# Gate and MLP modulation: from accumulated rows closed by TensorE to dot products closed on GpSimd

## The chip, the cores and the metric

The kernel runs on one NeuronCore of a Trainium2 chip. The metric is the device time of one execution in microseconds; the time before is the median of three runs. A profile holds one execution, taken by the hardware profiler; its rows name the engines PE (TensorE), PEld (TensorE's weight loads), DVE (VectorE), ACT (ScalarE), POOL (GpSimd) and SP (the queue that issues the DMAs).

## The reference, cut to what matters

One decoder block on 1024 tokens of width 1024, all in float32. A conditioning vector `c` modulates both sub-layers:

```python
cond = jax.nn.silu(c)
mod = cond @ w_ada + b_ada                     # 6 x 1024 values
sh_a, sc_a, gt_a, sh_m, sc_m, gt_m = split(mod, 6)
h = rms_norm(x, g_attn_pre) * (1 + sc_a) + sh_a
...                                            # projections, rotary, attention A and B, mixing
x = x + gt_a * rms_norm(mixed @ w_out, g_attn_post)
h = rms_norm(x, g_mlp_pre) * (1 + sc_m) + sh_m
y = square(relu(h @ w_up)) @ w_down
x = x + gt_m * rms_norm(y, g_mlp_post)
```

Attention A has 8 query heads on 2 key heads with a window of 128 and a sink; attention B has 8 heads that mix three dilated windows. Rotary turns the first 16 of each head's 64 columns. The change concerns the last four parts of `mod`: `gt_a` (needed when the attention's output is gated), `sh_m` and `sc_m` (needed before the MLP) and `gt_m` (needed at the very end), and the tables for the rotary turn.

## The kernel before, in words

TensorE's float32 products are made of three products of rounded high and low parts: every projection, output and MLP step is three 128x512 matmuls (L910, L911 and L913; L1818 to L1820; L2308 to L2310).

The work goes through these stages. At the start the first two parts of `mod` are computed and `x` is normed and transposed. Then come six units of projections, `pj`, two for attention A (`u` = 0 and 1) and four for B (`u` = 2 to 5). While the projections of one unit run, the attention of the units before runs in between: scores (`s_ps`), softmax with the largest value found on VectorE, the exponential on ScalarE (`p_sb`), the division mostly on GpSimd, transposes on TensorE (`pt_ps`), their split into high and low part on ScalarE and VectorE (`ph`), and the outputs (`o_ps`). In B units the third item of each head looks far back (`far`): it needs a regrouped copy of the queries (`q_far`, on ScalarE or GpSimd) and a chain of small VectorE operations (`st_far`, `a_far`, `d_far`, `z_far`). Then follow the output projection with gate and norm, and the MLP as seven products of a fast matrix scheme for each of eight halves.

The order of every engine's instructions is fixed when the program is written out. A planner (`Sched`) holds queues of steps with estimated durations, dependencies, and counted resources (`Res`) for buffers; it repeatedly hands out the step that can start first, ties by `prio`. Steps with two engines to choose from go where they end earlier. TensorE has named streams (`dense`, `s`, `t`, `pv`, `fin`, ...), and `dense` fills in where no attention step is ready. Each engine then executes its list strictly in order, so a step that waits holds up all behind it. The count `st.d` is the number of projection units done.

The modulation (`ada_piece`, L1035). The weights of the four parts form 8 halves of 512 columns. Each partition holds eight of the 1024 rows, and a piece takes two of these eight, so a half is 4 pieces. A piece is a load of 512 KB into a staging buffer (`stage`, 5 buffers, shared with the projections' `hl` tiles) and four GpSimd operations: each of the two rows times its value of `cond` (L1058, L1062), added to an accumulator `ada_acc` (L1063). After the fourth piece TensorE sums over the 128 partitions by a matmul with ones (stream `fin`): for the gates one 128x512 matmul (L1076), whose result VectorE adds to `b_ada` and multiplies by the gain, both loaded as 128 equal rows, and which goes to DRAM as 128 rows (`gate_d`); for `sh_m` and `sc_m` four matmuls with one column (L1079), closed by VectorE into `s_m` and `g_m`. A bank of PSUM is taken from `px` for it. The first 24 pieces (six halves) are let go one by one by `feed_ada` from `st.d` of 1.0 to 4.93; the last 8 pieces run on VectorE (L1060) during the MLP, let go by `feed_ada2`.

The rotary tables (`tables`, L735): GpSimd copies sines and cosines into a tile `rows` by small copies of 8 columns per token block (L748; 10 for each of the two tiles of the first call, 8 for each of the second), TensorE transposes them (`ptab`, L754), ScalarE scales them into `tabs`. The first call serves units 0 and 1; the second, let go when the projections of unit 2 begin, serves the B units.

Of the kernel before, what the change touches and what calls it, by code (L numbers as in the profile page):

```python
# [10 lines left out]
F32 = mybir.dt.float32  # L11
# [8 lines left out]
P = 128  # L20
# [28 lines left out]
_INS = ["x", "positions", "w_mod", "w_ada", "b_ada", "g_attn_post", "w_in", "w_out", "g_mlp_post", "w_up", "w_down"]  # L49
# [14 lines left out]
CW = CW_PK + 8  # L64
# [35 lines left out]
def _host(inputs):  # L100

    h = {n: np.ascontiguousarray(inputs[n]) for n in _INS if n != "w_mod"}
# [14 lines left out]
    h["w_mod"] = np.ascontiguousarray(w.transpose(3, 2, 4, 1, 0)).reshape(KC, 2, P, D)  # L117
    h["positions"] = np.ascontiguousarray(inputs["positions"][0].reshape(TB, P).T)
# [255 lines left out]
def hybrid_block(ctx: ExitStack, tc: tile.TileContext, x, positions, w_mod, w_ada, b_ada, g_attn_post, w_in, w_out,  # L374
                 g_mlp_post, w_up, w_down, consts, out):
# [4 lines left out]
    w_ada, w_out, w_up, w_down = w_ada[0], w_out[0], w_up[0], w_down[0]  # L380
# [57 lines left out]
    gate_d = [dram.tile([P, D], F32, name=f"gate_d{i}") for i in range(2)]  # L438
    ada_view = w_ada.rearrange("(p j) n -> p j n", j=KC)
# [40 lines left out]
    def rsqrt_mean(dst, src, deps, dur):  # L480
        box, n = [], dst.shape[-1]

        def first():
            box.append(small.tile([P, 8], F32, name="rs_t", tag="rs_t"))
# [111 lines left out]
    e_sin = op("ACT", 1.5, lambda: A.activation(small.tile([P, 8], F32, name="rs_t", tag="rs_t")[:, 0:1], ones[:, 0:1],  # L596
# [9 lines left out]
    condb, bc = p0.tile([P, D], F32, name="condb"), {}  # L606
# [128 lines left out]
    def tables(groups, place, r_place, r_bank, bank, deps):  # L735

        for i in range(2):
            b = {}

            def f_rows(i=i, b=b):  # L740
                t = b["t"] = place()[:].rearrange("p (b r) -> p b r", b=TB)
                G.memset(t, 0.0 if i else 1.0)
                for o, step, h in groups:
                    for x in range(2):
                        src = sinw[:, :, 1 - x] if i else cosw[:]
                        o_ = o + 64 * x
                        for j in range(h):
                            G.tensor_copy(t[:, :, o_ + j * step:o_ + j * step + (8 * h - h) * step + 1:h * step], src)  # L748
            e = op("POOL", 8.0 if r_place is r_wa else 4.4, f_rows, [e_rope], takes=[(r_place, 1)], prio=0)
            for x in range(2):  # L750
                def f_t(x=x, b=b):
                    b[x] = bank()
                    for j in range(4):
                        T.transpose(b[x][:, j], b["t"][:, 4 * x + j], ident)  # L754
                d = pe_op("tab", 0.43, f_t, [e], takes=[(r_bank, 1)], gives=[(r_place, 1)] if x else [])
                e_tab[x].append(op("ACT", t_ps(512) + AP_COST, lambda i=i, x=x, b=b: A.mul(
                    tabs[i][:, 512 * x:512 * x + 512], b[x][:].rearrange("p b t -> p (b t)"), scl[0]), [d] + deps[x],
                                   gives=[(r_bank, 1)], prio=2))
# [231 lines left out]
    def feed_proj():  # L990
        if len(sc.pe.get("dense", [])) <= 4 and todo_dense:
# [3 lines left out]
            if (u, x, c) == (2, 0, 0):  # L995
                for e_ in e_tab:
                    e_.clear()
# [6 lines left out]
    def open_attention():  # L1004
        if any(x.t is None for x in e_tab[0] + e_tab[1] + list(e_hl.values())):
            return False
        nonlocal kring, qring, vfring, pprob, pth, opool, adp, mask_a, mask_b, mask_n, mask_f, swap, pick, e_mask
# [9 lines left out]
        adp = pool("adp", 1, **kw)  # L1017
# [4 lines left out]
        e_mask = load(lambda: nc.sync.dma_start(masks[:], consts[:, CW_MB:CW]), 724992, prio=-20)  # L1022
        swap = [masks[:, 1152 + P * w:1152 + P * w + P] for w in range(2)]
        pick = [masks[:, 1408 + 4 * w:1412 + 4 * w] for w in range(2)]
        mask_b, mask_n = masks[:, 0:512], masks[:, 512:768]
        mask_f, mask_a = masks[:, 768:896], masks[:, 896:1152]
# [4 lines left out]
    kring = qring = vfring = pprob = pth = opool = adp = mask_a = mask_b = mask_n = mask_f = swap = pick = e_mask = None  # L1031
# [3 lines left out]
    NADA = 24  # L1035
    ada = Tok()
    ada.i, ada.acc, ada.e, ada.raw, ada.gate = 0, None, Ev(0.0), {}, {}
    e_mod = {}
    r_adacc = Res(1)

    def ada_piece(i, eng, accp, psum, r_ps, r_acc=None):
        g, jp = divmod(i, 4)
        col = 2 * D + g * 512

        def f_load():
            ada.raw[i] = stage("wa_st")
            nc.sync.dma_start(ada.raw[i][:].rearrange("p (j n) -> p j n", j=2),
                              ada_view[:, 2 * jp:2 * jp + 2, col:col + 512])
        el = load(f_load, 524288, takes=[(r_stg, 1)], prio=20)

        def f_acc():
            wa = ada.raw.pop(i)[:].rearrange("p (j n) -> p j n", j=2)
            if jp == 0:
                ada.acc = accp()
            for j in range(2):
                cj = cond[:, 2 * jp + j:2 * jp + j + 1]
                if jp == 0 and j == 0:
                    eng.tensor_scalar(ada.acc[:, :512], wa[:, 0], cj, 1.0, ALU.mult, ALU.mult)  # L1058
                elif eng is V:
                    V.scalar_tensor_tensor(ada.acc[:, :512], wa[:, j], cj, ada.acc[:, :512], ALU.mult, ALU.add)  # L1060
                else:
                    G.tensor_scalar(wa[:, j], wa[:, j], cj, 1.0, ALU.mult, ALU.mult)  # L1062
                    G.tensor_tensor(ada.acc[:, :512], ada.acc[:, :512], wa[:, j], ALU.add)  # L1063
# [3 lines left out]
        if jp < 3:  # L1067
            return
# [1423 lines left out]
```

## Time and profile before

| | |
|---|---|
| runs, us | 1094.43, 1095.38, 1095.84 (median 1095.38) |
| profiled execution, us | 1095.04 |
| its span, us | 1093.3 |
| granted TensorE clock, mean | 0.997 |
| DMA, bytes moved | 197.95 MB |

The span runs from the first to the last instruction that the profiler saw; 1.7 us of the execution lie around it. How to read the rows: a group has line, engine, operation, output and input, count, then busy time and mean ns, then the idle time before the group's instructions and what ended it. A wait row names who waited, for whom, us in total, times and longest. A timeline row has start, length, and in brackets the idle time before it. In the chain of work that ended last each step gets only the time that it adds to the chain.

### The profile page before, as it was taken

How to read it: one execution, taken by the hardware profiler on the slowest of the kernel's cores; microseconds unless marked ns; L12 is line 12 of the kernel's file. 1: busy time of each engine (PE TensorE's matmuls, PEld its weight loads, DVE VectorE, ACT ScalarE, POOL GpSimd, SP SyncE). 2: the span in 40 equal slices, each digit the busy share in tenths (PEclk: the TensorE clock that was granted, in tenths of full speed). 3: DMA queues.
4: the chain of work that ended last, by engine and by line, in shares of the span. 5: the costliest groups of instructions: out<-in, count | busy, mean ns of one | idle time of the engine just before them, and what ended most of it. 6: DMA issues, size and time to landing. Idle time of an engine off the chain costs nothing.

```text
span 1093.3 us, 15289 instructions
## 1 busy us (share of the span) xinstructions
PE 1077.9 (99%) x5254; PEld 898.1 (82%) x5254; DVE 815.7 (75%) x1430; ACT 621.8 (57%) x1155; POOL 284.3 (26%) x378
## 2 busy tenths in 40 slices
PE   8999999999999999999999999999999999999997
PEld 6888888888888888888888888888888888888885
DVE  7978776667768688699796655898746995537978
ACT  6868876455656867686755234733245632347532
POOL 3649778496846631100000000000000000000002
PEclk9999999999999999999999999999999999999999
DMA  8565656354625447368721579234687043594014
GB/s 341 212 228 154 190 170 210 138 183 141 206 102 173 142 149 267 116 231 313 278 82 39 178 254 356 89 99 145 246 302 295 1 135 119 192 330 177 29 47 185
DMA packets 90559, 197.95 MB, mean 181 GB/s; under 512 B 8560, under 2 KB 25072, under 8 KB 90480
## 3 DMA queue, kind: packets, MB, share of 16 engines
q1 hardware_dynamic: 90480, 196.95, 52.2%
q8 instruction: 42, 0.69, 0.3%
q14 instruction: 37, 0.30, 0.1%
HBM read 145.54 MB, written 32.51 MB: 163 GB/s over the span
## 4 chain that ended last, share of the span: by engine, by line
PE 94%; DVE 2%; POOL 2%; issue 1%; ACT 1%; DMA 1%; SPq 0%; POOLq 0%; DVEq 0%
PE mlp_ps L2308 19%; PE mlp_ps L2310 18%; PE mlp_ps L2309 18%; PE pj L910 5%; PE pj L913 5%; PE pj L911 5%; PE y_ps L1818 3%; PE y_ps L1819 3%; PE y_ps L1820 3%; PE o_ps L1517 2%; PE s_ps L1324 1%; PE s_ps L1229 1%; PE o_ps L1417 1%; PE pt_ps L1381 1%; PE pt_ps L1481 1%; PE acc L910 1%
## 5 line engine op out<-in xcount | busy, mean ns | idle before, releaser
L2308 PE MATMUL mlp_ps<-hw 128*128 128x512 f32 x896 | 349.6, 390 | 0.0
L2310 PE MATMUL mlp_ps<-hw 128*128 128x512 f32 x896 | 348.6, 389 | 0.0
L2309 PE MATMUL mlp_ps<-hw 128*128 128x512 f32 x896 | 348.6, 389 | 0.0
L2309 PEld LDWEIGHTS mlp_ps<-hw 128*128 128x128 f32 x896 | 168.2, 188 | 35.2 <-issue 0.5
L2308 PEld LDWEIGHTS mlp_ps<-hw 128*128 128x128 f32 x896 | 168.2, 188 | 35.2 <-issue 0.5
L2310 PEld LDWEIGHTS mlp_ps<-hw 128*128 128x128 f32 x896 | 168.2, 188 | 35.0
L2020 DVE TENSOR_TENSOR hw<-w,hw 128x1024 fp32r<-128x1024 f32 x92 | 109.9, 1221 | 83.2 <-ACT hw L2013 82.7
L2408 POOL TENSOR_TENSOR st<-st,nhalf 128x1 f32<-128x1 f32 x8 | 7.6, 956 | 611.0 <-DVE st L2405 611.0
L2013 ACT CAST hw<-w 128x1024 fp32r<-128x1024 f32 x92 | 93.6, 1049 | 122.6 <-PE mlp_ps L2310 90.3
L910 PE MATMUL pj<-hw,w_hl 128*128 128x512 f32 x240 | 102.4, 427 | 0.0
L913 PE MATMUL pj<-hw,w_hl 128*128 128x512 f32 x240 | 95.0, 396 | 0.0
L911 PE MATMUL pj<-hw,w_hl 128*128 128x512 f32 x240 | 94.7, 394 | 0.0
L2013 ACT CAST hw<-u 128x1024 fp32r<-128x1024 f32 x48 | 48.8, 1052 | 64.0 <-PE mlp_ps L2310 64.0
L2020 DVE TENSOR_TENSOR hw<-u,hw 128x1024 fp32r<-128x1024 f32 x48 | 57.1, 1220 | 17.2 <-ACT hw L2013 17.2
L2366 DVE TENSOR_TENSOR yacc<-yacc,mlp_ps 128x512 f32<-128x512 f32 x96 | 62.4, 684 | 4.5 <-PE mlp_ps L2310 4.3
L1063 POOL TENSOR_TENSOR ada_acc<-ada_acc,wa_st 128x512 f32<-128x512 f32 x42 | 55.2, 1314 | 3.5
L913 PEld LDWEIGHTS pj<-hw,w_hl 128*128 128x128 f32 x240 | 45.3, 189 | 10.3
L1818 PE MATMUL y_ps<-hw,oh 128*128 128x512 f32 x128 | 51.6, 403 | 0.0
L1819 PE MATMUL y_ps<-hw,oh 128*128 128x512 f32 x128 | 50.0, 391 | 0.0
L911 PEld LDWEIGHTS pj<-hw,w_hl 128*128 128x128 f32 x240 | 45.8, 191 | 4.4
L910 PEld LDWEIGHTS pj<-hw,w_hl 128*128 128x128 f32 x240 | 45.5, 190 | 4.5
L2347 ACT ACTIVATE u<-u 128x512 f32<-128x512 f32 x48 | 28.9, 625 | 30.9 <-DVE u L2345 30.2
(261 smaller groups left out, 1995.0 us busy)
## 6 DMA issues: line engine op xcount, KB each, us to landing
hw<-s_dram SPq DMA_DIRECT2D x84, 512.0 KB, 4.4
wa_st<-in_w_ada SPq DMA_DIRECT2D x32, 512.0 KB, 4.7
w<-in_w_up SPq DMA_DIRECT2D x32, 512.0 KB, 4.7
w<-in_w_down SPq DMA_DIRECT2D x32, 512.0 KB, 7.3
s_dram<-hw SPq DMA_DIRECT2D x28, 512.0 KB, 3.2
qt<-hl SPq DMA_DIRECT2D x40, 256.0 KB, 2.5
w_st<-in_w_in SPq DMA_DIRECT2D x36, 256.0 KB, 3.0
x_sb<-in_x SPq DMA_DIRECT2D x16, 512.0 KB, 6.0
```

The lines of the kernel that those rows point to most:

```text
L910: T.matmul(ps, w[:, 0, n], h[0], start=(k == 0), stop=False)
L911: T.matmul(ps, w[:, 1, n], h[0], start=False, stop=False)
L913: T.matmul(ps, w[:, 0, n], h[1], start=False, stop=(k == KC - 1))
L1063: G.tensor_tensor(ada.acc[:, :512], ada.acc[:, :512], wa[:, j], ALU.add)
L1818: T.matmul(ps[:], oh, wh[:, c0:c0 + 512], start=(k == 4 * m), stop=False)
L1819: T.matmul(ps[:], oh, wl[:, c0:c0 + 512], start=False, stop=False)
L2013: A.copy(out[j][0], flat(src[j]))
L2020: V.tensor_tensor(out[j][1], flat(src[j]), out[j][0].bitcast(F32), ALU.subtract)
L2308: T.matmul(ps[m][:], sh, mh, start=starts and k == 0, stop=False, **kw)
L2309: T.matmul(ps[m][:], sh, ml_, start=False, stop=False, **kw)
L2310: T.matmul(ps[m][:], sl, mh, start=False, stop=k == 3, **kw)
L2366: e = op("DVE", t_dv(512), lambda: V.tensor_tensor(y(), y(), ps[m][:], ALU.add), [e, ml.e_y[tb, n]], gives=gives, prio=-1 if (h, p) == ml. ...
```

## The change

The weights of the four parts are laid out by the host as 32 pieces of 128 partitions by 1024: a piece holds, for 128 of a part's 1024 outputs, one output per partition and its whole row of 1024 weights. The row form of `cond`, `condb`, which the start builds anyway, is kept in a pool that lives longer. A piece is now one load of 512 KB, two GpSimd products with `condb` of 512 columns each (L1052), and one ScalarE pass that copies in place and sums each row into a column of `dots` (L1057). After the eight pieces of a part, GpSimd closes it with operations on 128x8 (L1065 to L1074): adds the bias, multiplies by the gain (both now columns of the constants tile). The gates go to DRAM as one row of 1024 and are read back with every partition getting the same row. TensorE and VectorE have no part in it any more. All 32 pieces are let go between `st.d` of 2.0 and 5.29; the pieces in the MLP and the loads of biases and gains are gone.

In `tables` the copies that differ only by their place in a group become one copy with a broadcast; each copy is a step of its own, the transposes of the second call wait for the tables' last reader, and that call is let go two projections earlier, at the second projection of unit 1's second half. Several small tiles get fewer buffers (`rs_t` 3, `z_far` 1, `y_far` 1, `d_far` 2, `mn4` and `den4` 4, `rab` 2, `st2` 3, `st_l` 1).

```diff
-    NADA = 24
+    NADA = 4 * KC
...
-    def ada_piece(i, eng, accp, psum, r_ps, r_acc=None):
-        g, jp = divmod(i, 4)
-        col = 2 * D + g * 512
+    def ada_piece(i):
+        c, k = divmod(i, KC)
         def f_load():
             ada.raw[i] = stage("wa_st")
-            nc.sync.dma_start(ada.raw[i][:].rearrange("p (j n) -> p j n", j=2),
-                              ada_view[:, 2 * jp:2 * jp + 2, col:col + 512])
-        el = load(f_load, 524288, takes=[(r_stg, 1)], prio=20)
-        def f_acc():
...
-                    G.tensor_scalar(wa[:, j], wa[:, j], cj, 1.0, ALU.mult, ALU.mult)
-                    G.tensor_tensor(ada.acc[:, :512], ada.acc[:, :512], wa[:, j], ALU.add)
...
-                T.matmul(b[0][:, :512], ones[:], ada.acc[:, :512], start=True, stop=True)
-            else:
-                for k in range(4):
-                    T.matmul(b[0][:, k:k + 1], ada.acc[:, k * P:(k + 1) * P], ones[:, 0:1], start=True, stop=True)
...
+            nc.sync.dma_start(ada.raw[i][:], w_ada[c, k])
+        e = load(f_load, 524288, takes=[(r_stg, 1)], prio=20)
+        e = op("POOL", 2 * t_ptt(512), lambda: [G.tensor_tensor(ada.raw[i][:, cs], ada.raw[i][:, cs], condb[:, cs], ALU.mult)
+                                                for cs in (slice(0, 512), slice(512, D))], [e], prio=9)
+
+        def f_sum():
+            w = ada.raw.pop(i)[:]
+            A.activation(w, w, AF.Identity, accum_out=dots[:, c, k:k + 1])
+        ada.e.append(op("ACT", t_as(D) + 0.19, f_sum, [e], gives=[(r_stg, 1)], prio=9))
+        if k < KC - 1:
             return
...
+        def f_c():
+            d = dots[:, c]
+            if c == 1:
+                G.tensor_tensor(s_m[:], d, cols[:, 40:48], ALU.add)
+            elif c == 2:
+                G.tensor_tensor(g_m[:], d, b1m[:], ALU.add)
+                G.tensor_tensor(g_m[:], g_m[:], cols[:, 16:24], ALU.mult)
             else:
...
+                at = 16 if c else 0
+                G.tensor_tensor(d, d, gates[:, at:at + 8], ALU.add)
+                G.tensor_tensor(d, d, gates[:, at + 8:at + 16], ALU.mult)
+                if c:
+                    G.tensor_scalar(d, d, D ** 0.5, 1.0, ALU.mult, ALU.mult)
+        e = op("POOL", 0.3, f_c, ada.e + [e_mask], prio=4)
...
     def feed_ada():
-        if st.d > 1.0 + ada.i * 4.1 / NADA and ada.i < NADA:
+        if st.d > 2.0 + ada.i * 3.4 / NADA and ada.i < NADA:
...
     def tables(groups, place, r_place, r_bank, bank, deps):
...
-                        for j in range(h):
-                            G.tensor_copy(t[:, :, o_ + j * step:o_ + j * step + (8 * h - h) * step + 1:h * step], src)
-            e = op("POOL", 8.0 if r_place is r_wa else 4.4, f_rows, [e_rope], takes=[(r_place, 1)], prio=0)
+                    def f_rows(o=o + 64 * x, step=step, h=h, x=x, i=i, b=b):
+                        to = b["t"][:, :, o:o + (8 * h - 1) * step + 1:step].rearrange("p b (f j) -> p b f j", j=h)
+                        G.tensor_copy(to, (sinw[:, :, 1 - x] if i else cosw[:]).unsqueeze(3).to_broadcast([P, TB, 8, h]))
+                    e.append(op("POOL", 0.4 + 0.4 * h, f_rows, [es, e_rope], prio=0))
...
-            if (u, x, c) == (2, 0, 0):
+            if (u, x, c) == (1, 1, 1):
...
     def feed_ada2():
-        if ada.i < 32:
-            if ada.i >= NADA and ml.begun > 8 + 2 * (ada.i - NADA):
-                ada_piece(ada.i, V, lambda: stage("ada_acc"),
-                          lambda: px.tile([P, 512], F32, name="ada_ps", tag="x"), r_x, r_stg)
-                ada.i += 1
+        if ml.begun <= 24:
             return False
```

Where each engine's instructions stand before and after is shown with the prediction's steps.

More of the change, by code (lines that the diff above doesn't have):

```diff
@@ L100, in _host @@
 def _host(inputs):
-    h = {n: np.ascontiguousarray(inputs[n]) for n in _INS if n != "w_mod"}
+    h = {n: np.ascontiguousarray(inputs[n]) for n in _INS if n not in ("w_mod", "w_ada")}
     c = np.zeros((P, CW), np.float32)
@@ L594, in hybrid_block @@
     e = op("ACT", 0.1, lambda: A.activation(cond[:], c_raw, AF.Exp, scale=-1.0), [e_c], prio=0)
-    e_sin = op("ACT", 1.5, lambda: A.activation(small.tile([P, 8], F32, name="rs_t", tag="rs_t")[:, 0:1], ones[:, 0:1],
+    e_sin = op("ACT", 1.5, lambda: A.activation(small.tile([P, 8], F32, name="rs_t", tag="rs_t", bufs=3)[:, 0:1], ones[:, 0:1],
                                                 AF.Sin), [e, e_init], prio=0)
@@ L738, in tables, with f_set @@
             b = {}
[L740 to L746, printed above, removed]
-                        for j in range(h):
-                            G.tensor_copy(t[:, :, o_ + j * step:o_ + j * step + (8 * h - h) * step + 1:h * step], src)
-            e = op("POOL", 8.0 if r_place is r_wa else 4.4, f_rows, [e_rope], takes=[(r_place, 1)], prio=0)
+            def f_set(i=i, b=b):
+                b["t"] = place()[:].rearrange("p (b r) -> p b r", b=TB)
+                G.memset(b["t"], 0.0 if i else 1.0)
+            es = op("POOL", 1.0, f_set, [e_rope], takes=[(r_place, 1)], prio=3)
+            e = []
+            for o, step, h in groups:
+                for x in range(2):
+                    def f_rows(o=o + 64 * x, step=step, h=h, x=x, i=i, b=b):
+                        to = b["t"][:, :, o:o + (8 * h - 1) * step + 1:step].rearrange("p b (f j) -> p b f j", j=h)
+                        G.tensor_copy(to, (sinw[:, :, 1 - x] if i else cosw[:]).unsqueeze(3).to_broadcast([P, TB, 8, h]))
+                    e.append(op("POOL", 0.4 + 0.4 * h, f_rows, [es, e_rope], prio=0))
             for x in range(2):
@@ L1723, in f_set @@
             def f_set():
-                A.activation(small.tile([P, 8], F32, name="rs_t", tag="rs_t")[:, 0:1], ones[:, 0:1], AF.Sqrt)
+                A.activation(small.tile([P, 8], F32, name="rs_t", tag="rs_t", bufs=3)[:, 0:1], ones[:, 0:1], AF.Sqrt)
             op("ACT", 1.5, f_set, [e_x2[1]], prio=3)
@@ L1855, in f1 @@
             def f1():
-                t = small.tile([P, 8], F32, name="rs_t", tag="rs_t")
+                t = small.tile([P, 8], F32, name="rs_t", tag="rs_t", bufs=3)
                 bx.append(t)
@@ L1909, in f_ev @@
                 return f
[L1910 removed]
+            e = op(("DVE", "ACT"), (1.3, 1.45), (f_ev(V), f_ev(A)), [et[kg]] + [e_mod[g] for g in (1, 2)] +
                    (e_h2[q][-1:] if tq else []) + ([e_far] if tb == 0 else []),
```

127 lines of the change are left out of this document (42 added, 85 removed).

## The prediction, made before the changed kernel ran

> **What bounds the kernel now.** I read the page first (busy shares and the chain of work that ended last), then the waits of TensorE, then busy time by stretches. The page:
>
> ```profile
> span 1093.3 us, 15289 instructions
> PE 1077.9 (99%) x5254; PEld 898.1 (82%) x5254; DVE 815.7 (75%) x1430; ACT 621.8 (57%) x1155; POOL 284.3 (26%) x378
> PE 94%; DVE 2%; POOL 2%; issue 1%; ACT 1%; DMA 1%; SPq 0%; POOLq 0%; DVEq 0%
> ```
>
> TensorE is busy in 1077.9 of 1093.3 us and holds 94% of the chain. Whatever leaves its queue shortens the run, unless a wait takes its place. The waits of TensorE after the start are these (line waited at, releaser, us in total, times, longest):
>
> ```profile
> PE o_ps L1517 <- DVE ph L1497: 1.3, 1, 1.3
> PE pm_o L1776 <- DVE ph L1497: 1.0, 1, 1.0
> PE s_ps L1229 <- POOL q_far L1205: 0.8, 1, 0.8
> PE ada_ps L1079 <- POOL p_sb L1299: 0.2, 1, 0.2
> ```
>
> Only the last two fall where the change works. Busy time by stretches (length; PE, PEld, DVE, ACT, POOL; granted clock; DMA share; GB/s):
>
> ```profile
> 80.00:140.00 60.00, 60.00 (x349) 51.00 (x348) 46.78 (x139) 50.73 (x145) 49.92 (x88) 1.00 0.58 168
> 138.00:326.00 188.00, 187.03 (x1068) 159.90 (x1067) 130.98 (x390) 110.79 (x300) 134.93 (x162) 0.99 0.52 163
> 190.00:200.00 10.00, 9.40 (x52) 8.17 (x53) 4.98 (x17) 3.71 (x13) 8.37 (x9) 0.83 0.19 59
> 420.00:1080.00 660.00, 660.00 (x2941) 546.49 (x2940) 491.75 (x564) 337.61 (x477) 13.78 (x17) 1.00 0.50 179
> ```
>
> From 80 to 140 us ScalarE is 85% busy (50.73 of 60) and TensorE never waits; in the MLP (420 to 1080) it never waits either. At 190 us the 0.80 us wait is followed by a granted clock of 0.83 over 10 us, 1.7 us lost.
>
> **What the change takes off TensorE.** Each of the eight modulation halves ends in matmuls against ones. The instructions that write ada_ps, their count, minimum, median and maximum ns:
>
> ```profile
> L1079 PE MATMUL ada_ps<-ones,ada_acc x32: 164/250/250, 191.6 to 306.8; 128*128 128x1 f32 x32
> L1076 PE MATMUL ada_ps<-ada_acc,ones x8: 590/592/627, 106.8 to 781.1; 128*128 128x512 f32 x8
> ```
>
> Durations overlap in the pipeline, so I price them by the chain of waits, which gives each step only the time that it adds (start, us, what):
>
> ```profile
> 106.92 0.86 PE ada_ps L1076 x2
> 148.19 0.86 PE ada_ps L1076 x2
> 191.79 0.79 PE ada_ps L1079 x8
> 306.25 0.79 PE ada_ps L1079 x8
> 631.02 0.89 PE ada_ps L1076 x2
> 631.91 0.23 PE mlp_ps L2308
> 780.87 0.86 PE ada_ps L1076 x2
> ```
>
> The MLP matmul behind one takes its usual 0.23 us, so nothing is given back. Four row closings at 0.86, 0.86, 0.89 and 0.86 are 3.47 us; four column closings at the 0.79 of their first and last are 3.16. Together 6.63 us leave a queue that is never empty. In the program, TensorE in the fourth B unit, where s_ps are scores, o_ps outputs and pj a projection, before:
>
> ```order
> L1408 MATMUL o_ps<-ph,v_hl 128x128
> L1229 MATMUL s_ps<-kt,qt 128x256 x4
> L1079 MATMUL ada_ps<-ones,ada_acc 128x1 x4
> L910 MATMUL pj<-hw,w_hl 128x512
> L911 MATMUL pj<-hw,w_hl 128x512
> ```
>
> The same place after the change, with shifted lines; its first five rows are
>
> ```order
> L1374 MATMUL o_ps<-ph,v_hl 128x128
> L1195 MATMUL s_ps<-kt,qt 128x256 x4
> L916 MATMUL pj<-hw,w_hl 128x512
> L917 MATMUL pj<-hw,w_hl 128x512
> L919 MATMUL pj<-hw,w_hl 128x512
> ```
>
> The closing is gone and the projection follows the scores. The counts of scores, transposes and outputs behind the last projection are the same in both programs (32, 44, 60), so the attention's end has the same work to hide.
>
> **What it adds in the B units.** The 24 GpSimd pieces of before run from 82 to 304 us (L1063); their loads are let go from 1.0 to 1.0 + 23 x 4.1/24 = 4.93 units, so a unit lasts about 57 us, and the new gate (2.0 to 5.29) puts 32 pieces into about 138 to 326 us. GpSimd's additions with their first and last start, its groups (busy, mean ns, idle before), and the modulation's part between 138 and 326 us, that is of L1058, L1062 and L1063 in this order:
>
> ```profile
> L1063 POOL TENSOR_TENSOR ada_acc<-ada_acc,wa_st x42: 1278/1294/1817, 82.1 to 304.3; 128x512 f32<-128x512 f32 x42
> L1063 POOL TENSOR_TENSOR ada_acc<-ada_acc,wa_st 128x512 f32<-128x512 f32 x42 | 55.2, 1314 | 3.5
> L1062 POOL TENSOR_SCALAR wa_st<-wa_st,cond 128x512 f32<-128x512 f32 x42 | 31.4, 747 | 20.7 <-DMA wa_st<-in_w_ada 20.7
> L1315 POOL COPY p_sb<-nsink 128x4 f32<-128x4 f32 x16 | 2.9, 192 | 1.8 <-PE pt_ps L1381 1.8
> 138.00:326.00 188.00, 0.00 (x0) 3.34 (x4) 0.99 0.52 163
> 138.00:326.00 188.00, 23.26 (x31) 0.99 0.52 163
> 138.00:326.00 188.00, 41.63 (x32) 0.99 0.52 163
> ```
>
> There the modulation takes 68.2 us now (3.34 + 23.26 + 41.63). It will take 64 x 1.314 = 84.1, and eight closing operations of 128x8, put at the 0.19 us of the 128x4 copy (1.5 us; at the 1.31 of a product, 10.5). GpSimd goes from 134.9 to 134.9 - 68.2 + 85.6 = 152.3 of 188 us, 81%. ScalarE gets 32 sums; an ACTIVATE of 1024 columns with a sum beside it, and the read of the sum:
>
> ```profile
> L1849 ACT ACTIVATE junk<-y_sb 128x1024 bf16<-128x1024 f32 x14 | 14.8, 1059 | 8.0 <-DVE y_sb L1842 3.7 <-DVE y_sb L1868 2.9 <-DVE rs_t L1786 1.3
> L1849 ACT ACTIVATION_READ_ACCUMULATOR junk<-y_sb 128x1 f32 x14 | 2.7, 193 | 0.0
> ```
>
> 1.059 + 0.193 = 1.25 us, 40 us in all: ScalarE goes from 110.8 to 150.8 of 188 us, 80%, under the 85% that it bore from 80 to 140 us without a wait of TensorE. Both fit; what counts is order. ScalarE in the first B unit, where ph are the probabilities that TensorE waits for, p_sb the softmax, w_hl the next weights, before:
>
> ```order
> L1388 CAST ph<-pt_ps 128x512 [waits PE_49,Activation_49]
> L561 CAST w_hl<-w_st 128x512 [waits DMAHW5_49]
> L1187 ACTIVATE p_sb,den<-p_sb,mn 128x384 [waits DVE_49,Pool_49]
> L561 CAST w_hl<-w_st 128x512 [waits DMAHW4_49,PE_49]
> L1452 COPY otmp<-o_ps 64x512 [waits PE_49,Activation_49]
> ```
>
> and after, where L1057 is the sum:
>
> ```order
> L1354 CAST ph<-pt_ps 128x512 [waits PE_49,Activation_49]
> L1057 ACTIVATE wa_st,dots<-wa_st 128x1024 [waits DMAHW6_49,DMAHW3_49,Pool_49]
> L566 CAST w_hl<-w_st 128x512 [waits DMAHW3_49,PE_49]
> L1153 ACTIVATE p_sb,den<-p_sb,mn 128x384 [waits DVE_49]
> L1418 COPY otmp<-o_ps 64x512 [waits PE_49,Activation_49]
> ```
>
> So ScalarE now waits for a GpSimd product, which waits for a load, with softmax, ph and otmp queued behind, and TensorE waits for those. How late a product can be is bounded by what GpSimd and ScalarE waited for before:
>
> ```profile
> POOL ada_acc L1058 <- DMA wa_st<-in_w_ada: 10.1, 3, 5.6
> POOL wa_st L1062 <- DMA wa_st<-in_w_ada: 20.7, 7, 9.8
> ACT hl L798 <- POOL ada_acc L1063: 2.4, 1, 2.4
> ```
>
> GpSimd stood 30.8 us before loads, ScalarE 2.4 us behind a modulation block, and TensorE is charged with one 0.80 us wait for it. New waits of TensorE thus lie between -2.7 us (0.80, 0.17 and the clock's 1.7 vanish) and the rivals' 7.8 and 13.1. I take +1.0, near the 0.80 that is charged now: each block gets shorter (2.6 us for a product against 4.1 for a piece of two multiplications and two additions), but the pieces are more and ScalarE is tied to them.
>
> **A rule against the change.** Products with two tensor inputs can hold up VectorE. The row where a 128x16 operation takes 2.19 us while GpSimd works on a 2.39 us product, and what TensorE then waits:
>
> ```profile
> 330.33 2.39 POOL L1591 TENSOR_TENSOR hw<-wo_st,hw 128x1024 fp32r<-128x1024 f32 x1
> 330.57 2.19 DVE L1289 TENSOR_TENSOR st_far<-st_far,d_far 128x16 f32<-128x16 f32 x1
> 333.92 0.56 PE L1517 MATMUL o_ps<-ph,v_hl 128*128 128x256 f32 x3 [1.30 <-DVE ph L1497]
> ```
>
> The Trainium skill, page "SBUF — State Buffer", section "SBUF: two separate sides", says why: a VectorE operation with two SBUF inputs and a GpSimd operation exclude each other for a whole instruction. By that rule the trace agrees: both rows end within 0.05 us. The change doubles such holds in the B units, 41.6 to 84.1 us, in pieces of 1.31. Yet between 80 and 320 us no wait of TensorE is put down to VectorE with the 41.6, so it is inside my +1.0; at full price it is rival (b), 1096.2.
>
> **Edits put at nothing.** The wider rotary copies: GpSimd's first 20 copies last 6.66 + 8.06 us, and TensorE's wait before the transposes is 0.35, not put down to them:
>
> ```profile
> 28.28 6.66 POOL L748 COPY rows<-cosw 128x64 f32<-128x64 f32 x10
> 38.25 8.06 POOL L748 COPY rows<-sinw 128x64 f32<-128x64 f32 x10
> 54.63 0.63 PE L754 MATMUL ptab<-head,rows 128*128 128x128 f32 x4 [0.35 <-issue]
> ```
>
> so at most 0.35 us comes of it; if a wide copy were no faster than four narrow ones, the projections still cover it. The eight VectorE pieces leave the MLP, where VectorE is not waited for. The gate rows become a load from one row; used far later. Fewer buffers for small tiles: their next writer stands several items behind; cover gone, one reuse would cost about the 0.8 of a late operand.
>
> **The sum.** 1095.04 for the profiled execution (span 1093.3), less 6.63, plus 1.0: 1089.4 us. The median of the runs is 1095.38, 0.34 above this execution; I leave that out.
>
> **The rivals.** (a) The present waits go too: 1095.04 - 6.63 - 2.7 = 1085.7. For it: the wait at 190 us came from GpSimd running two blocks before q_far. Against: pieces stand before q_far still. (b) The holds: if each of the six far items in the stretch costs TensorE the 1.30 us seen once, 7.8 us: 1096.2. (c) The freed time in the attention turns into waits for the softmax chain, and only the two MLP closings count, 0.89 + 0.86: 1093.3. Against: projections fill TensorE there, 187.03 of 188 us. (d) The slower one: ScalarE, in order behind late products. If ten of 32 (as ten times GpSimd waited for a load) cost TensorE 0.80 us each, and three of these the clock's 1.7, it is 8.0 + 5.1 = 13.1: 1101.5. It decides from 6.63 + 2.2 = 8.8 us of new waits, 0.28 per piece. For it: the new order; against: 30.8 us of waiting cost TensorE 0.97 before.
>
> **How the numbers follow.** Chances: forecast 0.59, (a) 0.13, (b) 0.10, (c) 0.06, (d) 0.12. A measurement can tell 0.2%, 2.2 us: faster is below 1093.2 (forecast and a, 0.72), same up to 1097.6 (b and c, 0.16), slower above (d, 0.12). The range goes from 1085.0, under (a), to 1096.2, (b); it leaves out (d). The forecast's own range is 1087 to 1092.
>
> **What would show it.** Right: no ada_ps rows, TensorE's busy time down by about 6.6 us, waits of TensorE between 130 and 330 us of 1 to 4 us, the MLP without waits. Wrong: waits of ph, p_sb or otmp on ScalarE for wa_st that TensorE shows again, granted clock under 0.97 in several stretches of 10 us, or VectorE's far operations at 1 us and more with TensorE behind them.

## The result, and the profile after

The changed kernel takes 1088.98 us (median of 6 runs, 1088.14 to 1093.14) beside 1095.61 us of the kernel before (median of 6). The ratio is 0.995, with a 95% interval from 0.9939 to 0.9961: 4.3 to 6.7 us. The profiled execution took 1089.32 us, 5.72 less than the one of before.

The page of the changed kernel:

```profile
span 1087.5 us, 15255 instructions
PE 1071.9 (99%) x5214; PEld 893.5 (82%) x5214; DVE 802.7 (74%) x1397; ACT 649.8 (60%) x1208; POOL 275.0 (25%) x349
PE 95%; DVE 2%; POOL 1%; ACT 1%; issue 1%; POOLq 0%; DVEq 0%; ACTq 0%
```

TensorE has 40 matmuls fewer (5214 against 5254) and is busy 6.0 us less. Its idle time is span less busy: 15.4 us before, 15.6 after. So in this pair of profiles the whole gain stands in the busy row, and the idle time is the same in sum. A second profile of the changed kernel, `after_again` below, has 17.6 us of idle time, so differences of 2 us in it are not told apart. Its waits after the first 70 us (line waited at, releaser, us in total, times, longest):

```profile
PE pm_o L1742 <- DVE ph L1463: 1.0, 1, 1.0
PE x_far L1231 <- DVE ph L1463: 0.8, 1, 0.8
PE o_ps L1483 <- DVE ph L1463: 0.8, 1, 0.8
PE x_far L1231 <- DVE z_far L1224: 0.8, 1, 0.8
```

They add up to 3.4 us, as the four of before did to 3.3, but only the one at pm_o is the same. The waits at q_far and ada_ps are gone, and so is the hold that the prediction shows, 1.30 us at 333.92 us; in their place stand two at x_far (198.80 and 266.94 us) and one at o_ps (219.73), each 0.8 us. So the B units lost and the stretch behind them won: by stretches TensorE's idle time goes from 0.97 to 2.31 us between 138 and 326 us, and from 2.51 to 1.19 us between 326 and 420. Busy time by stretches (length; PE, PEld, DVE, ACT, POOL; granted clock; DMA share; GB/s), the last two rows being two short stretches:

```profile
80.00:140.00 60.00, 60.00 (x356) 51.57 (x355) 45.70 (x136) 49.79 (x136) 33.41 (x64) 1.00 0.36 109
138.00:326.00 188.00, 185.69 (x1055) 158.24 (x1054) 135.33 (x392) 143.38 (x363) 151.35 (x170) 1.00 0.61 203
420.00:1080.00 660.00, 659.41 (x2939) 546.36 (x2937) 482.56 (x553) 334.86 (x475) 15.64 (x19) 1.00 0.47 169
190.00:200.00 10.00, 9.23 (x56) 7.92 (x55) 8.60 (x26) 7.79 (x24) 8.69 (x7) 1.00 0.24 74
380.00:390.00 10.00, 10.00 (x54) 8.48 (x54) 7.63 (x12) 5.67 (x9) 4.49 (x8) 0.86 0.35 115
```

GpSimd is busy 151.35 of the 188 us of the B units and ScalarE 143.38, and TensorE still works 185.69 of them. The clock's dip stands at 380 us instead of 190 us, at about the same price: 1.4 us for 1.7. In after_again no stretch of 10 us between 70 and 430 us has one, so it comes and goes between executions of one kernel. The groups of the modulation (busy us, mean ns of one, idle before it):

```profile
L1052 POOL TENSOR_TENSOR wa_st<-wa_st,condb 128x512 f32<-128x512 f32 x64 | 82.2, 1307 | 24.8 <-DMA wa_st<-in_w_ada 21.4 <-issue 3.4
L1057 ACT ACTIVATE wa_st<-wa_st 128x1024 f32<-128x1024 f32 x32 | 33.9, 1059 | 17.5 <-POOL wa_st L1052 17.5
```

The durations are those that the rows of before gave, and ScalarE does stand behind products, 17.5 us in all. The three waits of the B units show what that and the holds of VectorE do here. Two are holds (start, us, what, in brackets the idle time before it):

```profile
194.92 2.54 POOL L1052 TENSOR_TENSOR wa_st<-wa_st,condb 128x512 f32<-128x512 f32 x2
196.29 2.45 DVE L1224 TENSOR_TENSOR z_far<-st_far,masks 128x32 f32<-128x32 f32 x2
198.80 0.41 PE L1231 MATMUL x_far<-z_far,masks 128*128 128x32 f32 x2 [0.77 <-DVE z_far L1224]
263.86 2.42 DVE L1224 TENSOR_TENSOR z_far<-st_far,masks 128x32 f32<-128x32 f32 x2 [1.09 <-ACT p_sb L1214]
266.94 0.63 PE L1231 MATMUL x_far<-z_far,masks 128*128 128x32 f32 x4 [0.78 <-DVE ph L1463]
```

Two VectorE operations of 128x32 (0.18 us each where nothing holds them) take 2.45 us, while the products run; TensorE stands 0.77 us for their result. At 263.86 us the same happens beside two products (2.53 us from 263.70); the `ph` that TensorE waits for stands behind the held pair in VectorE's order. The third wait comes of ScalarE, in order behind a late product:

```profile
214.36 2.55 POOL L1052 TENSOR_TENSOR wa_st<-wa_st,condb 128x512 f32<-128x512 f32 x2 [5.44 <-DMA wa_st<-in_w_ada]
216.95 1.06 ACT L1057 ACTIVATE wa_st<-wa_st 128x1024 f32<-128x1024 f32 x1 [2.38 <-POOL wa_st L1052]
218.00 0.39 ACT L1153 ACTIVATE p_sb<-p_sb,mn 128x128 f32<-128x128 f32 x1
218.39 0.56 ACT L1460 CAST ph<-pt_ps 128x512 fp32r<-128x512 f32 x1
218.51 0.16 DVE L1156 RECIPROCAL den<-den 128x1 f32<-128x1 f32 x1 [2.59 <-ACT p_sb L1153]
218.98 0.69 DVE L1463 TENSOR_TENSOR ph<-pt_ps,ph 128x512 fp32r<-128x512 f32 x1 [0.31 <-ACT ph L1460]
219.73 0.90 PE L1483 MATMUL o_ps<-ph,v_far 128*64 128x128 f32 x8 [0.77 <-DVE ph L1463]
```

A load comes 5.44 us late and ScalarE waits 2.38 us for the product. The softmax and the high part of `ph` stand behind the sum, VectorE waits 2.59 us for the softmax and then makes the low part of `ph`, and TensorE stands 0.77 us for that. Both mechanisms of the rivals (b) and (d) are there. In this profile they make all 2.3 us of TensorE's waits in the B units, less than 1 us at a time.

### The profile page after: what moved, and what is told of

The parts are those of the page before. It is cut to its first block, busy times and chain, and to the rows that moved or that the text cites. A ratio compares the mean times of both kernels' runs of the same rounds, so it can differ in the third digit from the quotient of the medians.

```text
span 1087.5 us, 15255 instructions
## 1 busy us (share of the span) xinstructions
PE 1071.9 (99%) x5214; PEld 893.5 (82%) x5214; DVE 802.7 (74%) x1397; ACT 649.8 (60%) x1208; POOL 275.0 (25%) x349
## 4 chain that ended last, share of the span: by engine, by line
PE 95%; DVE 2%; POOL 1%; ACT 1%; issue 1%; POOLq 0%; DVEq 0%; ACTq 0%
PE mlp_ps L2275 19%; PE mlp_ps L2276 19%; PE mlp_ps L2274 19%; PE pj L916 5%; PE pj L919 5%; PE pj L917 5%; PE y_ps L1784 3%; PE y_ps L1786 3%; PE y_ps L1785 3%; PE o_ps L1483 2%; PE s_ps L1195 1%; PE s_ps L1290 1%; PE o_ps L1383 1%; PE pt_ps L1347 1%; PE pt_ps L1447 1%; PE acc L916 1%
## 5 line engine op out<-in xcount | busy, mean ns | idle before, releaser
L1052 POOL TENSOR_TENSOR wa_st<-wa_st,condb 128x512 f32<-128x512 f32 x64 | 82.2, 1307 | 24.8 <-DMA wa_st<-in_w_ada 21.4
```

Source lines behind the costliest of these rows:

```text
L1052: e = op("POOL", 2 * t_ptt(512), lambda: [G.tensor_tensor(ada.raw[i][:, cs], ada.raw[i][:, cs], condb[:, cs], ALU.mult) for cs in (slice(0 ...
```

## The experiments

The theory: the gain is the eight closings that left a full TensorE queue, and the new work stays hidden as long as GpSimd and ScalarE have room. Rivals: the gain comes from the other edits; only the two closings in the MLP count; holds or late products eat part of a larger gain. Every variant starts from the changed kernel and is timed in five rounds beside the kernel before on its own chip, so the ratios are what can be compared. The changed kernel's own runs go from 1086.5 to 1093.5 (both sets), so steps under some 2 us are not told apart. A variant that gives the planner other steps or other estimates is planned anew: in no_products, short_sums, dve_dots, gate_in_mlp, old_rows and the two with closings, steps may stand in another order or on another engine than in the changed kernel. Only wide_products, the doubled runs and memset_load keep its estimates.

| variant | median us | ratio to before, 95% |
|---|---|---|
| the changed kernel | 1088.98 | 0.995 (0.9939 to 0.9961) |
| the same again, after_again | 1090.44 | 0.9954 (0.9937 to 0.9971) |
| closings_back | 1096.26 | 1.001 (1.000 to 1.002) |
| mlp_closings_back | 1091.62 | 0.9968 (0.9952 to 0.9985) |
| old_rows | 1089.89 | 0.9963 (0.995 to 0.9977) |
| wide_products | 1088.50 | 0.995 (0.9937 to 0.9962) |
| no_products | 1089.89 | 0.9963 (0.995 to 0.9976) |
| short_sums | 1088.76 | 0.9952 (0.9938 to 0.9965) |
| dve_dots | 1090.18 | 0.9965 (0.9952 to 0.9979) |
| gate_in_mlp | 1089.56 | 0.9957 (0.9942 to 0.9971) |
| double_sums | 1103.06 | 1.0067 (1.0054 to 1.008) |
| double_products | 1160.89 | 1.0581 (1.0558 to 1.0604) |
| memset_load | 1185.62 | 1.0826 (1.0812 to 1.0841) |

**closings_back** puts eight closings on TensorE again; nothing reads them.

```diff
+        def f_fin():
+            t = px.tile([P, 512], F32, name="ada_ps", tag="x")
+            if c in (0, 3):
+                T.matmul(t[:], ones[:], condb[:, 0:512], start=True, stop=True)
+            else:
+                for n in range(4):
+                    T.matmul(t[:, n:n + 1], condb[:, n * P:(n + 1) * P], ones[:, 0:1], start=True, stop=True)
+        if k % 4 == 3:
+            pe_op("fin", 0.86 if c in (0, 3) else 0.45, f_fin, [e], takes=[(r_x, 1)], gives=[(r_x, 1)])
```

> The changed kernel with eight closings put back on TensorE: after every fourth piece a 128x512 matmul with ones (gates) or four matmuls with one column (shift and scale), on condb, with no reader; all of them in the B units. Theory of the path (the gain is the closings that left a full TensorE queue): 6.6 us more than the changed kernel's 1089.0, so 1095.6, at least 1094. Rival (the gain comes from the re-spread pieces, the tables or the relief of VectorE): at most 1091.

Measured: a ratio of 1.001, all of the gain gone. TensorE's busy row and the closings' own rows in its trace:

```profile
PE 1079.6 (99%) x5254; PEld 898.4 (82%) x5254; DVE 805.2 (73%) x1400; ACT 650.4 (59%) x1208; POOL 269.0 (25%) x346
L1061 PE MATMUL ada_ps<-ones,condb x32: 165/250/251, 200.1 to 281.2; 128*128 128x1 f32 x32
L1058 PE MATMUL ada_ps<-condb,ones x8: 590/592/592, 172.3 to 336.4; 128*128 128x512 f32 x8
```

The same 40 matmuls, now all between 172 and 337 us and with the products and sums still on the other engines, cost the 0.006 in ratio (1.001 - 0.995), 6.6 us; by an estimate from the two intervals, taken as independent, it is known to some 1.6 us either way. By the profiles the loss stands in TensorE's busy time, 7.7 us more than after, and not in its idle time (16.1 us for 15.6). That is the term of the prediction, put back.

**mlp_closings_back** puts only two 128x512 closings into the MLP, where two of the eight stood before.

```diff
+    def mlp_fin():
+        def f_fin():
+            t = px.tile([P, 4, P], F32, name="ada_ps", tag="x")
+            T.matmul(t[:], ones[:], ones[:].unsqueeze(1).to_broadcast([P, 4, P]), start=True, stop=True)
+        pe_op("fin", 0.86, f_fin, [], takes=[(r_x, 1)], gives=[(r_x, 1)])
...
+        if ada.fin < 2 and ml.begun > (14, 22)[ada.fin]:
+            ada.fin += 1
+            mlp_fin()
```

> The changed kernel with two 128x512 matmuls with ones put back on TensorE in the MLP alone, with no reader. Theory of the path: 2 x 0.87, so 1090.7. Rival (c) of the prediction, by which only the MLP's closings count and freed time in the attention turns into waits: the whole gain goes with these two, 1095. If closings cost nothing anywhere: 1089.0.

Measured: 0.9968, so 0.0018 or 2.0 us above the changed kernel where two closings were priced at 1.75; the intervals overlap, so this run alone would not settle it. Its busy row:

```profile
PE 1073.7 (98%) x5218; PEld 892.6 (82%) x5218; DVE 806.4 (74%) x1397; ACT 650.0 (60%) x1208; POOL 274.5 (25%) x349
```

TensorE has 1.8 us more than after, not 6. With closings_back, rival (c) falls: closings in the attention count as much as those in the MLP.

**old_rows** undoes the rotary copies, their dependencies and their place in the program.

```diff
-                        G.tensor_copy(to, (sinw[:, :, 1 - x] if i else cosw[:]).unsqueeze(3).to_broadcast([P, TB, 8, h]))
+                        for j in range(h):
+                            G.tensor_copy(t[:, :, o_ + j * step:o_ + j * step + (8 * h - h) * step + 1:h * step], src)
...
-            if (u, x, c) == (1, 1, 1):
+            if (u, x, c) == (2, 0, 0):
```

> The changed kernel with the rotary tables as before: many narrow copies, second call at the start of unit 2. Theory of the path: the copies lie beside other work, so within 1 us of 1089.0. Rival (the tables carry part of the gain, by the start's wait or by GpSimd's time in the A units): 1091 or more.

Measured: 0.9963 against 0.995, 1.4 us with overlapping intervals. A share of that size for the tables is possible and can't be told; they do not carry the gain.

**wide_products** makes one product of 1024 columns out of two of 512.

```diff
-        e = op("POOL", 2 * t_ptt(512), lambda: [G.tensor_tensor(ada.raw[i][:, cs], ada.raw[i][:, cs], condb[:, cs], ALU.mult)
-                                                for cs in (slice(0, 512), slice(512, D))], [e], prio=9)
+        e = op("POOL", 2 * t_ptt(512), lambda: G.tensor_tensor(ada.raw[i][:], ada.raw[i][:], condb[:], ALU.mult), [e], prio=9)
```

> The changed kernel with one GpSimd product of 1024 columns per piece in place of two of 512; the order is nearly the same. Theory of the holds (a product keeps VectorE's two-input operations out for its whole length): single operations of z_far, st_far, d_far up to 2.4 us, waits of TensorE between 130 and 330 us of 3 us and more against 2.3, so 1090 to 1094. If holds don't matter to the end: 1089.0 or, with one dispatch less per piece, a little under.

Measured: 0.995, the changed kernel's own ratio. The operation that the holds strike most, with its least, median and longest ns:

```profile
L1223 DVE TENSOR_TENSOR z_far<-st_far,masks x16: 177/331/1690, 196.3 to 371.7; 128x32 f32<-128x32 f32 x16
```

One of them is held up to 1.69 us, against 1.32 in the kernel after and 1.87 in after_again, so this operation shows no effect of the size. VectorE's longest `w_hl` addition does: 2.72 us beside products of 2.40 us, for 1.66 and 1.58 us beside those of 1.31. The end does not move (the 1090 to 1094 of the theory of holds missed): the size of the pieces carries nothing here that can be told.

**no_products** leaves the products out.

```diff
-        e = op("POOL", 2 * t_ptt(512), lambda: [G.tensor_tensor(ada.raw[i][:, cs], ada.raw[i][:, cs], condb[:, cs], ALU.mult)
-                                                for cs in (slice(0, 512), slice(512, D))], [e], prio=9)
```

> The kernel after without GpSimd's 64 products: ScalarE sums the weights as loaded, so the six modulation parts are wrong sums; loads, sums, closings and everything else stay. It takes the holds of VectorE and the lateness of products (theories b and d) away altogether. Path theory: TensorE's waits in the B units of the kernel after are three, 2.3 us together, so at most 2.3 us come of it: 1086.5 to 1090, TensorE's busy time within 1 us of 1071.9. If holds or late products cost more than the waits show (by a slower clock, or hidden in other operations), it comes out at 1085 or under. VectorE's far operations of 128x32 should fall from up to 2.45 us to under 0.8 us.

Measured: 0.9963, no faster than with them. Its busy row, the B units, and the operation that was held:

```profile
PE 1071.7 (98%) x5214; PEld 892.1 (82%) x5214; DVE 786.7 (72%) x1387; ACT 649.9 (60%) x1207; POOL 205.0 (19%) x297
138.00:326.00 188.00, 184.85 (x1041) 156.33 (x1040) 116.59 (x374) 140.37 (x360) 81.39 (x117) 1.00 0.60 202
L1222 DVE TENSOR_TENSOR z_far<-st_far,masks x16: 181/184/237, 197.3 to 374.3; 128x32 f32<-128x32 f32 x16
L571 DVE TENSOR_TENSOR w_hl<-w_st,w_hl 128x512 fp32r<-128x512 f32 x11 | 7.8, 713 | 2.9 <-ACT w_hl L566 2.9
```

GpSimd falls by 70 us and VectorE by 16.0 (786.7 for 802.7). Not all of the 16.0 had been holds. The planner now gives ten steps of VectorE to the freed GpSimd, six `w_hl` additions among them (11 here, 17 in the kernel after); counted at their mean durations, that is some 9 us by an estimate. The rest, some 7 us, is time in which VectorE had been held: the 16 z_far operations alone take 2.3 us for 9.5. TensorE is busy 1071.7 us for 1071.9. So the holds are real, and taking them away brings no gain that can be told; the newly planned order has waits of its own (184.85 us busy in the B units), so they are not shown to cost nothing.

**short_sums** shortens the sums to 8 of 1024 columns.

```diff
-            A.activation(w, w, AF.Identity, accum_out=dots[:, c, k:k + 1])
-        ada.e.append(op("ACT", t_as(D) + 0.19, f_sum, [e], gives=[(r_stg, 1)], prio=9))
+            A.activation(w[:, 0:8], w[:, 0:8], AF.Identity, accum_out=dots[:, c, k:k + 1])
+        ada.e.append(op("ACT", 0.4, f_sum, [e], gives=[(r_stg, 1)], prio=9))
```

> The kernel after with ScalarE's 32 sums cut from 1024 columns to 8 (the rest of each sum is left out, so the modulation is wrong): 32 x 0.9 = some 29 us leave ScalarE, its order behind the products stays. Path theory: ScalarE's load does not reach TensorE, 1087 to 1090. If ScalarE's 40 us cost TensorE anything beyond the single 2.59 us row seen (theory d in a milder form), 1085 to 1087.

Measured: 0.9952. The B units:

```profile
138.00:326.00 188.00, 186.23 (x1053) 158.17 (x1053) 133.44 (x394) 122.29 (x365) 147.96 (x170) 1.00 0.59 203
```

ScalarE does 21 us less in the stretch, and nothing that can be told comes of it.

**dve_dots** does product and sum of a piece in one VectorE operation.

```diff
-        e = op("POOL", 2 * t_ptt(512), lambda: [G.tensor_tensor(ada.raw[i][:, cs], ada.raw[i][:, cs], condb[:, cs], ALU.mult)
-                                                for cs in (slice(0, 512), slice(512, D))], [e], prio=9)
...
-            A.activation(w, w, AF.Identity, accum_out=dots[:, c, k:k + 1])
-        ada.e.append(op("ACT", t_as(D) + 0.19, f_sum, [e], gives=[(r_stg, 1)], prio=9))
+            V.tensor_tensor_reduce(w, w, condb[:], 1.0, 0.0, ALU.mult, ALU.add, dots[:, c, k:k + 1])
+        ada.e.append(op("DVE", t_dv(D) + 0.16, f_sum, [e], gives=[(r_stg, 1)], prio=9))
```

> The kernel after with product and sum of a piece in one VectorE operation (tensor_tensor_reduce over 1024 columns), nothing on GpSimd and ScalarE for it but the closings. VectorE takes some 32 x 1.2 = 38 us more between 138 and 326 us, where it is busy 143 to 135 of 188 us, so some 174 of 188. Path theory (only what TensorE waits for counts): VectorE makes the probabilities' scaling and the far operands that TensorE waits for, and at over 90% it comes late: 2 to 10 us of new waits, 1091 to 1099. If the engine that does the work does not matter so long as TensorE's queue is relieved: 1089 within 1.5.

Measured: 0.9965, 1.6 us above the changed kernel with overlapping intervals. The 1091 to 1099 of my theory missed. The B units and the new operation:

```profile
138.00:326.00 188.00, 186.28 (x1059) 158.98 (x1058) 151.46 (x444) 112.62 (x301) 98.52 (x124) 1.00 0.59 204
L1055 DVE CUSTOM_DVE_ANT_0 wa_st<-wa_st,condb 128x1024 f32<-128x1024 f32 x32 | 40.9, 1277 | 9.0 <-DMA wa_st<-in_w_ada 9.0
```

I had put VectorE at 174 of 188 us; it is at 151.46. The 40.9 us came as expected, but they stand on a VectorE that is freed of the products' holds and gives steps to GpSimd (116.59 us in no_products), not on the 135.33 of the kernel after. GpSimd is at 98.52 us here for 81.39 there.

**gate_in_mlp** moves the last eight pieces into the MLP, with the tiles that they need kept until then.

```diff
-    NADA = 4 * KC
+    NADA = 3 * KC
...
-        if ml.begun <= 24:
+        if ada.i < 32 and ml.begun > 8 + 2 * (ada.i - NADA) and ada.i >= NADA:
+            ada_piece(ada.i)
+            ada.i += 1
+        if ada.i < 32 or 3 not in e_mod:
             return False
```

> The kernel after with 24 of the 32 pieces in the B units and the last part's eight in the MLP, on GpSimd and ScalarE as before, which stand nearly idle there; no work on TensorE for it. The pieces in the B units get a third more room each. Path theory: only a part of the 2.3 us of waits in the B units can go, and the MLP, whose TensorE queue is full, hides the rest: 1087 to 1090. If the density of the pieces in the B units costs more than its waits show: 1086 or under. If loads and products in the MLP collide with its weight loads or hold VectorE: a wait of TensorE in the MLP and 1091 or more.

Measured: 0.9957. The B units and the MLP:

```profile
138.00:326.00 188.00, 185.84 (x1055) 157.76 (x1054) 131.92 (x393) 134.18 (x345) 134.24 (x154) 1.00 0.54 180
420.00:1080.00 660.00, 658.95 (x2935) 546.05 (x2933) 492.53 (x554) 342.17 (x490) 45.51 (x38) 1.00 0.49 175
```

GpSimd has 17 us more room in the B units, and TensorE uses none of it. No variant is measurably faster than the changed kernel: whatever lightens GpSimd or ScalarE there moves the end by nothing that can be told from some 2 us.

So the load was raised instead, in the same order of instructions. **after_again** is the changed kernel beside them.

> The kernel after once more, unchanged, so that the others of this set have it on their own chip: 1088 to 1091.

Measured: 0.9954. Its busy row and the B units:

```profile
PE 1072.2 (98%) x5214; PEld 891.4 (82%) x5214; DVE 806.9 (74%) x1397; ACT 649.5 (60%) x1208; POOL 273.8 (25%) x349
138.00:326.00 188.00, 183.37 (x1027) 154.18 (x1026) 135.87 (x380) 140.20 (x357) 149.22 (x164) 1.00 0.61 200
```

With a span of 1089.8 us TensorE is idle for 17.6 us, and its listed waits between 130 and 330 us are 4.3 us, the longest of 1.80 us again behind a sum that stood 2.48 us for its product. So the same program has 2 us more of waits there than in the first profile. The runs of higher load, on this chip or another, are compared with this one.

**double_sums** does each sum twice.

```diff
-            A.activation(w, w, AF.Identity, accum_out=dots[:, c, k:k + 1])
+            for _ in range(2): A.activation(w, w, AF.Identity, accum_out=dots[:, c, k:k + 1])
```

> The kernel after with each ScalarE sum done twice, in the same order: 32 x 1.25 = 40 us more, 151 to 191 of the 188 us. If ScalarE's load reaches TensorE once it is full (probabilities, softmax, weight conversions behind the sums): new waits for ph, hw or p_sb, 1092 to 1105. If GpSimd alone sets the pace and ScalarE has slack by its long lead: within 2 of the kernel after.

Measured: 1.0067 against 0.9954 beside it, 12.6 us slower than the changed kernel (1103.06 for 1090.44). The B units:

```profile
138.00:326.00 188.00, 178.35 (x987) 146.81 (x986) 124.37 (x356) 164.41 (x395) 142.71 (x157) 1.00 0.57 187
```

ScalarE is at 164.41 of 188 us, 87%, and TensorE loses 5.0 us more in the stretch than in after_again (178.35 for 183.37). Over the whole span (1101.3 us) it is idle 23.6 us for 17.6 and busy 5.5 us longer with the same matmuls; where these 5.5 us come from isn't traced. So a cost shows at 87% that can't be told at 75 to 76% (140.20 and 143.38), before the engine is full. Doubling also makes all that stands behind a sum some 1.06 us later, and load and lateness are not separated here.

**double_products** does each product twice.

```diff
-                                                for cs in (slice(0, 512), slice(512, D))], [e], prio=9)
+                                                for cs in (slice(0, 512), slice(512, D)) * 2], [e], prio=9)
```

> The kernel after with each GpSimd product done twice in the same place, in the same order (the second multiplies again, so the modulation is wrong): 64 x 1.3 = 83 us more for GpSimd, 151 to 234 of the 188 us. This is theory d at a dose that cannot fit. If only what TensorE waits for counts and a full GpSimd reaches it (softmax scalings and far operands in order behind products): more than 8.8 us of new waits between 138 and 400 us, 1098 to 1120. If the pieces merely stretch past 326 us and TensorE's own queue hides them: within 2 of the kernel after.

Measured: 1.0581, 70 us slower than the changed kernel, more than the 1098 to 1120 that I had expected. The B units, and TensorE's longest wait with what stood before it:

```profile
138.00:326.00 188.00, 148.06 (x740) 122.06 (x739) 126.45 (x276) 102.21 (x260) 158.34 (x163) 0.88 0.43 147
273.50 16.75 DVE L571 TENSOR_TENSOR w_hl<-w_st,w_hl 128x512 fp32r<-128x512 f32 x1
276.74 1.25 POOL L1158 TENSOR_SCALAR p_sb<-p_sb,den 128x384 f32<-128x384 f32 x2
277.95 4.94 POOL L1052 TENSOR_TENSOR wa_st<-wa_st,condb 128x512 f32<-128x512 f32 x4
282.83 1.99 POOL L1171 CAST q_far<-qt 128x1024 fp32r<-128x1024 f32 x1
284.78 4.92 POOL L1052 TENSOR_TENSOR wa_st<-wa_st,condb 128x512 f32<-128x512 f32 x4
290.17 1.01 DVE L1358 TENSOR_TENSOR ph<-pt_ps,ph 128x384 fp32r<-128x384 f32 x2
290.77 0.58 PE L1370 MATMUL o_ps<-ph,v_hl 128*128 128x256 f32 x1 [10.27 <-DVE ph L1358]
291.10 0.68 DVE L571 TENSOR_TENSOR w_hl<-w_st,w_hl 128x512 fp32r<-128x512 f32 x1
```

A VectorE addition of 128x512, 0.68 us when it comes again at 291.10, takes 16.75 while GpSimd works without a gap, and ends at 290 us, where the gap comes. TensorE stands 10.27 us behind it. With as many operations as in after_again (1397), VectorE is busy 33 us longer over the span (840.0 for 806.9), 19 us of that in its `w_hl` additions. GpSimd's share of the stretch is 84% (158.34 of 188), hardly more than the 81% of the kernel after: a share alone does not tell that an engine has become the limit. The Trainium skill, page "SBUF — State Buffer", section "SBUF: two separate sides", says that the loser is shut out for the whole instruction of the winner; here the trace goes further, since the addition, which began beside four products (5.03 us from 271.73), then sat through a chain of eleven GpSimd operations from 276.74 us on (eight products, two scalings, a conversion) and did not get in between two of them.

That left open whether the 70 us come of holds (b) or of lateness (d). **memset_load** puts other work behind each piece's products: fills, which have no input.

```diff
+    junkp = const.tile([P, 8], F32, name="junkp")
...
                                                 for cs in (slice(0, 512), slice(512, D))]
+               + [G.memset(junkp[:], 0.0) for _ in range(26)], [e], prio=9)
```

> The kernel after with 26 fills of 128x8 on GpSimd behind each piece's two products, written to a small tile that nothing reads, in the order of the doubled products: 32 x 26 x 0.1 = 83 us more of GpSimd's time, as much as the second products took, but reading nothing from SBUF and holding no VectorE operation. If a late GpSimd made the 71 us of the doubled products (theory d), it comes out at 1140 or more; if the holds of VectorE made them (theory b), at 1100 or less, with VectorE's w_hl additions under 2.5 us instead of up to 16.75. In between, both.

Measured: 1.0826, 95 us above the changed kernel by the ratios. Its fills, the VectorE addition of above, the B units, and what ScalarE and TensorE wait for:

```profile
L1055 POOL MEMSET junkp<- 128x8 f32 x806 | 84.4, 105 | 44.7
L572 DVE TENSOR_TENSOR w_hl<-w_st,w_hl 128x512 fp32r<-128x512 f32 x8 | 5.5, 694 | 1.8 <-ACT w_hl L567 1.7
138.00:326.00 188.00, 147.64 (x702) 119.64 (x700) 91.72 (x265) 98.67 (x253) 153.25 (x657) 0.87 0.39 129
ACT wa_st L1059 <- POOL junkp L1055: 102.5, 28, 6.8
PE s_ps L1197 <- POOL q_far L1173: 11.3, 3, 4.7
PE pv L873 <- ACT vt L867: 8.8, 3, 5.9
```

The dose was not the equal one that I had put down: 806 of the 832 fills stand in the row, which goes from 138 to 460 us; over the whole span all of them take 87.1 us, with another 46.1 of gaps between them, 133 us. The second products took 79 (161.9 us for 128 products, 83.1 for after_again's 64). The fills add no holds: the eight `w_hl` additions there take 694 ns each for the 3315 of the doubled products, and VectorE is busy 800.8 us in all, no more than in after_again (806.9). The products that stayed still hold it, a z_far up to 1.86 us (1.87 in after_again). So lateness without added holds makes 95 us over the changed kernel, 95/133 = 0.71 for each microsecond added; the doubled products made 70/79 = 0.89. ScalarE stands 102.5 us behind GpSimd, 28 times, with the softmax and the weights behind it: mechanism (d). In double_products it stands behind it too, 65.0 us in 23 waits. By an estimate that takes the cost to grow evenly with the dose, lateness would make 0.71 x 79 = 56 of the 70 us. What exactly the holds add there stays open, since the doses differ; the wait of 10.27 us stands behind one.

## Why the prediction was right, step by step

**The removed closings.** Put at 6.63 us. TensorE's busy time fell by 6.0 us in the one profile and 5.7 in after_again's, and closings_back returned 6.6 us, give or take 1.6. The mechanism was right, and so was the size as far as the runs can tell; the instructions' own durations would have given 12.7 us (8 x 0.592 + 32 x 0.25), so the price by the chain of waits (0.79 and 0.86) was the better one.

**The waits.** Put at +1.0 us. TensorE's idle time went from 15.4 us to 15.6 in the one profile and 17.6 in the other, +0.2 and +2.2, so the term is of the right size and no run fixes it closer than 2 us. What it is made of was not foreseen. In the B units new waits did come (idle 0.97 to 2.31 us), nearly the +1.0; but the prediction kept the wait of 1.30 us at 333.92, and this one went. The clock's loss, 1.7 us before, is 1.4 in the first profile and none in after_again. That the two waits cancel in the first profile is luck, and so is the agreement of 1089.4 with 1089.32: single runs of the changed kernel go from 1086.5 to 1093.5. The waits between 130 and 330 us are 2.3 us in the first profile, inside the 1 to 4 named, and 4.3 in after_again, just outside. No ada_ps rows are left, and the MLP has no listed wait.

**Loads of the engines.** GpSimd was put at 152.3 of 188 us and is at 151.35; ScalarE was put at 150.8 and is at 143.38. For the sums themselves, 1.059 + 0.193 held (1059 ns in the group above). 31 of the 32 fall into the stretch; the rest of the difference is other work that stands elsewhere and isn't traced. "Both fit" was right in that no lighter load was measurably faster. The prediction's reason for ScalarE, the 85% that it bore from 80 to 140 us, is neither shown nor refuted: doubled sums cost 12.6 us at 87%, just above it, and no run lies between 76% and 87%. That stretch also has another work on it.

**The closings on GpSimd** were put at 0.19 us each. Two of their rows:

```profile
L1067 POOL TENSOR_TENSOR g_m<-dots,b1m 128x8 f32<-128x8 f32 x1 | 1.0, 965 | 0.0
L1071 POOL TENSOR_TENSOR dots<-dots,masks 128x8 f32<-128x8 f32 x2 | 0.4, 197 | 0.0
```

All eight are as put (191 to 206 ns), but for one of 965 ns, which takes 200 ns in no_products.

**Rival (b)** had the right mechanism and the wrong price: the holds are there, some 7 us of VectorE's time, and two of TensorE's waits (0.77 and 0.78 us) stand behind one, 1.55 us in all for the 7.8 put down, and taking them all away gains nothing that can be measured. **Rival (c)** fell with closings_back. **Rival (d)** is what happens when the load is raised: 12.6 us with doubled sums, 95 with fills. At the load of this change it reached TensorE with one wait of 0.77 us in the first profile and one of 1.80 us in after_again. **Rival (a)** was half there: the wait at q_far and the dip at 190 us did go, but in the first profile others took their place.

**Edits put at nothing.** The tables lie within 1.4 us or so by old_rows. The gate rows, the smaller pools and VectorE's relief in the MLP were not tried apart; closings_back holds all of them and is no faster than before, so together with the new waits they carry nothing that can be told. Whether a gain and a loss among them cancel stays open.

## What to carry to other kernels

Where one engine's queue is never empty, price an edit by what it adds to or takes from that queue, and take the price from the chain of waits, not from pipelined durations. Work on the other engines is free only while they have room: here lightening them gained nothing, and doubling ScalarE's sums, from 75% to 87% of the stretch, cost 12.6 us. To learn how near that point is, double the suspected cost as well as taking it away.

## What the runs showed beside that

A VectorE addition of two SBUF inputs can be shut out for as long as GpSimd works without a gap (16.75 us for 0.68), not for one instruction only. An idle TensorE costs more than its waits when they are many: in double_products and memset_load the granted clock of the B units is 0.88 and 0.87, with 1.00 in the kernel after. Over the whole span of double_products TensorE is idle 47 us longer than in after_again (65.0 for 17.6) and busy 24 us longer with the same matmuls (1096.3 for 1072.2); in memset_load it is 55 and 41 us. A single wait may or may not bring a dip. The one of 0.97 us at pm_o, which ends at 376.93 us in the kernel after, comes with 0.86 from 380 to 390 us; the same wait of 0.97 us in the kernel before (up to 382.92 us) and of 0.96 us in after_again (up to 380.68 us) comes with none, nor do those of 0.77 us at 198 and 219 us in the kernel after.
